# The last RMS statistic: its root moved from GpSimd to ScalarE and VectorE, its final products all on VectorE

## The chip, the core and the metric

One core of a Trainium2 chip runs the whole program. The metric is the time of one execution on the device in microseconds (us), the median of several runs. Engines are TensorE (PE; its weight loads are PEld), VectorE (DVE), ScalarE (ACT), GpSimd (POOL) and SyncE (SP, which issues most DMAs). Each engine works through its own list of instructions in order; semaphores hold an instruction back until what it needs from another engine is done.

## What is computed

One step of a two-layer network on 640 tokens (512 latent, 128 context) of width 1024. Each layer has a token mixer (attention, then a gated linear recurrence) and a SwiGLU block, each with an RMS norm in front and a gated residual behind. This case is about the very end: the down-projection of the last block, its residual, and the final RMS norm of every token:

```python
def _rms_norm(x, g):
    xf = x.astype(jnp.float32)
    y = xf * lax.rsqrt(jnp.mean(xf * xf, axis=-1, keepdims=True) + RMS_EPS)
    return (y * g.astype(jnp.float32)).astype(x.dtype)
...
        lat = lat + g2_l[:, None, :] * f_l
    y_prompt = _rms_norm(ctx, final_g)
    y_sample = _rms_norm(lat, final_g)
```

## The kernel before

The residual stream `x` is kept with features on the 128 partitions: 8 feature chunks (`KT = 8`) by 640 tokens. A mean over features is thus a sum over partitions and over the 8 chunks. ScalarE squares each chunk, the squares are added up chunk by chunk in `ssq`, and `stat` (line 376) lets TensorE multiply the sum by a column of ones: tokens come out on partitions, one column per block of 128 tokens (tile `at`). The last squares are not added but given to the same matmuls as further parts (`lastq`). VectorE makes `var` of it (divide by 1024, add epsilon), GpSimd raises it to the power -0.5 (`rs`, line 389), VectorE spreads the result on a diagonal (`dg`), and TensorE multiplies the diagonal by a square of ones, which puts the root of each token on all partitions, in PSUM (tile `mx`, line 394).

`project_last` (line 451) is the tail. It takes the tokens in two chunks, a (0 to 384) and b (384 to 640). For a it runs the 8 products of TensorE with the down weights, one for each feature chunk, with residual (line 425) and square (line 371), then `stat`. For b it runs the 8 products again; beside them the final products of a (`final`, line 465) are placed, each of them `x` times gain times root. In b, ScalarE squares each chunk (line 477, tiles `ssq` and `snap`), GpSimd adds the squares of chunks 1 to 5 (line 479), and those of 6 and 7 go into the statistic as parts. ScalarE also scales chunks 6 and 7 of b by the gain (line 482). After b's `stat`, ScalarE copies the root out of PSUM (`g`, line 490), because GpSimd can't read there; VectorE does the final products of chunks 0 to 5 of b (line 497), GpSimd those of 6 and 7 (line 499). Stores to HBM go from SyncE's queue in pairs of feature chunks (`store`, line 468): four of a (384 KB each) and four of b (256 KB each).

Which instruction stands where in an engine's list is decided by a scheduler from the program's order and its dependencies; `tc.issue_after(i)` keeps an instruction behind `i`. All engines end at line 1205, the end of the program: each runs a DRAIN and then a barrier. ScalarE works with one table of functions at a time; a function of another table needs an ACT_TABLE_LOAD first, which the build puts in by itself.

Of the kernel before, what the change touches and what calls it, by code (L numbers as in the profile page):

```python
# [9 lines left out]
F32 = mybir.dt.float32  # L10
F32R = mybir.dt.float32r
AF = mybir.ActivationFunctionType
ALU = mybir.AluOpType
AX = mybir.AxisListType

P = 128
D = 1024
KT = D // P
# [22 lines left out]
HT = NTOK // 2  # L41
# [84 lines left out]
class _Step:  # L126
# [235 lines left out]
    def square(self, k, t0, t1):  # L362
        nc = self.nc
        s = slice(t0, t1)
        if k == 0:
            if t0 == 0:
                self.ssq = self.t([P, NTOK], F32, "ssq", 1, self.sb)
            nc.scalar.activation(self.ssq[:, s], self.x[:, k, s], AF.Square)
            return
        q = self.t([P, 384], F32, "sq", 2, self.sb)[:, :t1 - t0]  # L370
        nc.scalar.activation(q, self.x[:, k, s], AF.Square)
        if k < KT - 1:
            nc.vector.tensor_tensor(self.ssq[:, s], self.ssq[:, s], q, ALU.add)
        self.lastq[t0] = [q]

    def stat(self, t0, t1):
        nc = self.nc
        bl = [min(b, t1 - P) for b in range(t0, t1, P)]
        n = len(bl)
        ps = self.ps()  # L380
        parts = [(self.ssq, 0)] + [(q, t0) for q in self.lastq.get(t0, ())]
        for i, (q, o) in enumerate(parts):
            for j, b in enumerate(bl):
                self.at = nc.tensor.matmul(ps[:, j:j + 1], q[:, b - o:b - o + P], self.ones[:, 0:1], start=i == j == 0,
                                           stop=i == len(parts) - 1, skip_group_check=True).ins
        v = self.t([P, 8], F32, "var", 2)[:, 0:n]
        self.var = nc.vector.tensor_scalar(v, ps[:, 0:n], 1.0 / D, EPS, ALU.mult, ALU.add).ins  # L387
        r = self.t([P, 8], F32, "rs", 2)[:, 0:n]
        self.pw = nc.gpsimd.tensor_tensor(r, v, self.mhalf.broadcast_to([P, n]), ALU.pow).ins  # L389
        dg = self.t([P, 4, P], F32, "dg", 1, self.sb)[:, 0:n]  # L390
        self.dg = nc.vector.tensor_tensor(dg, self.ident.unsqueeze(1).broadcast_to([P, n, P]), r.unsqueeze(2).broadcast_to([P, n, P]), ALU.mult).ins
        ps = self.ps("rr" if "rr" in self.ptags else "mx")
        for j, b in enumerate(bl):
            mm = nc.tensor.matmul(ps[:, b - t0:b - t0 + P], self.ones, dg[:, j], start=True, stop=True)
        self.r = ps, t0
        return mm.ins
# [54 lines left out]
    def project_last(self, w, hi, lo, gk):  # L451
        nc, tc = self.nc, self.tc
        G = self.need(self.gcols, gk)
        us = []
        for f in range(0, KT, 2):
            us += self.two(w[f:f + 2], f % 4)
        (a0, a1), (b0, b1) = CHL
        for f, u in enumerate(us):
            self.residual(f, a0, a1, self.chunk(u, hi, lo, a0, a1), G, True)
        mm = self.stat(a0, a1)  # L460
        r0 = self.r[0][:, 0:a1 - a0]

        def final(k):
            xs = self.x[:, k, a0:a1]
            nc.vector.scalar_tensor_tensor(xs, xs, self.col("fg", k), r0, ALU.mult, ALU.mult)

        def store(k, t0, t1):
            nc.sync.dma_start(self.o["y"][k * P - P:k * P + P, t0:t1].rearrange("(k p) t -> p k t", p=P), self.x[:, k - 1:k + 1, t0:t1])

        squares = []  # L470
        for f, u in enumerate(us):
            with tc.issue_after(mm) if f == KT - 1 else nullcontext():
                ps = self.chunk(u, hi, lo, b0, b1)
            last = self.residual(f, b0, b1, ps, G, False)
            xs = self.x[:, f, b0:b1]
            q = self.ssq[:, b0:b1] if f == 0 else self.t([P, HT], F32, "snap", 3, self.sb)[:, 0:b1 - b0]
            nc.scalar.activation(q, xs, AF.Square)
            if 0 < f < KT - 2:
                nc.gpsimd.tensor_tensor(self.ssq[:, b0:b1], self.ssq[:, b0:b1], q, ALU.add)
            squares.append(q)  # L480
            if f >= KT - 2:
                nc.scalar.activation(xs, xs, AF.Copy, scale=self.col("fg", f))
            if 1 < f < KT - 1:
                with tc.issue_after(last):
                    final(f - 2)
        self.lastq[b0] = squares[KT - 2:]
        self.stat(b0, b1)
        r1 = self.r[0][:, 0:b1 - b0]
        rs = self.t([P, HT], F32, "g", 3, self.sb)[:, 0:b1 - b0]
        nc.scalar.copy(rs, r1)  # L490
        with tc.issue_after(self.dg):
            for k in range(KT - 3, KT):
                final(k)
        for k in range(KT):
            xs = self.x[:, k, b0:b1]
            if k < KT - 2:
                nc.vector.scalar_tensor_tensor(xs, xs, self.col("fg", k), r1, ALU.mult, ALU.mult)
            else:
                nc.gpsimd.tensor_tensor(xs, xs, rs, ALU.mult)
        for k in (1, 3):  # L500
            store(k, a0, a1)
        for t0, t1, ks in ((b0, b1, (1,)), (a0, a1, (5, 7)), (b0, b1, (3, 5, 7))):
            for k in ks:
                store(k, t0, t1)
# [704 lines left out]
```

## Time and profile before

| | |
|---|---|
| time, median of 3 runs | 1558.96 us (1558.88 to 1559.05) |
| time of the profiled execution | 1559.64 us |
| its span, first to last instruction of the program | 1557.9 us |
| mean granted clock of TensorE | 0.982 |
| busy: PE, DVE, ACT, POOL | 1491.1, 1076.2, 719.0, 214.0 us |

A row of a timeline is: start and length in us, engine, line, operation, output tile <- input tiles, shapes, count of merged instructions, and in brackets the engine's idle time before it with what ended it. A row of a group is: line, engine, operation, tiles, shapes, count | busy us, mean ns of one | idle time before and its releaser. A row of one line's instructions has the count, then the shortest, median and longest duration in ns, then the first and the last start in us. An engine's name with a small q (SPq, POOLq) is the engine's sequencer, which runs DMA issues, waits and the DRAINs at the program's end.

### The profile page before, as it was taken

To read this page: it belongs to the slowest core of one execution; us is meant where nothing else is said; L and a number is where in the kernel's file an instruction comes from. 1 tells how busy PE (TensorE), PEld (TensorE's weight loads), DVE (VectorE), ACT (ScalarE), POOL (GpSimd) and SP (SyncE) were. 2 spreads that over 40 slices of the span, in tenths; PEclk is the share of its full clock that TensorE was granted. 3 is DMA by queue.
4 is the path that set the end of the run, shared out by engine and by line. 5 is a ranking of instruction groups with operands and counts; after the bars stand their busy time and mean duration, and the time that the engine had idled before them with its cause. 6 is when DMAs were issued, how large, how long until landed. Compare 5 with 4: busy or idle time off the path is not lost.

```text
span 1557.9 us, 26058 instructions
## 1 busy us (share of the span) xinstructions
PE 1491.1 (96%) x10307; PEld 1444.9 (93%) x10307; DVE 1076.2 (69%) x2035; ACT 719.0 (46%) x1329; POOL 214.0 (14%) x238
## 2 busy tenths in 40 slices
PE   6999999989999999999999999969989999999996
PEld 4899999879999999999999888869989999999996
DVE  5678788959999886444446489875876666555645
ACT  4576667654332123212334389764634342424232
POOL 2211122100111110000000000000132323232311
PEclk8999999999999999999999999989999999999998
DMA  9545655535666663222223112124242231313111
GB/s 377 157 114 165 178 167 164 154 122 188 189 191 189 203 194 116 71 82 82 62 84 114 62 58 72 55 97 152 70 142 70 82 109 55 109 55 109 55 55 68
DMA packets 69754, 188.25 MB, mean 121 GB/s; under 512 B 7793, under 2 KB 23297, under 8 KB 69505
## 3 DMA queue, kind: packets, MB, share of 16 engines
q1 hardware_dynamic: 57824, 144.49, 29.5%
q0 software_dynamic: 11520, 41.95, 8.7%
q8 instruction: 81, 1.33, 0.3%
q14 instruction: 41, 0.33, 0.1%
q10 hardware_dynamic: 288, 0.16, 0.0%
HBM read 171.09 MB, written 8.92 MB: 116 GB/s over the span
## 4 chain that ended last, share of the span: by engine, by line
PE 80%; DVE 8%; ACT 7%; DMA 2%; issue 2%; POOL 0%; SPq 0%; DVEq 0%; POOLq 0%; ACTq 0%
PE mm L210 13%; PE mm L209 13%; PE mm L211 13%; PE mx L211 5%; PE mx L210 5%; PE mx L209 5%; PE mx L819 3%; PE mx L821 3%; PE mx L820 3%; PE op L665 2%; PE tp L589 2%; PE mc L819 1%; PE mc L820 1%; PE mc L821 1%; DVE big L1057 1%
## 5 line engine op out<-in xcount | busy, mean ns | idle before, releaser
L209 PE MATMUL mm<-big,whi 128*128 128x320 f32 (+2 forms) x1290 | 402.4, 315 | 16.4 <-ACT big L1056 9.1
L210 PE MATMUL mm<-big,whi 128*128 128x320 f32 (+2 forms) x1290 | 405.0, 314 | 1.7 <-DVE big L1057 1.3
L211 PE MATMUL mm<-big,wlo 128*128 128x320 f32 (+2 forms) x1290 | 403.7, 314 | 1.2 <-DVE wlo L178 1.2
L209 PEld LDWEIGHTS mm<-big,whi 128*128 128x128 f32 x1290 | 245.3, 191 | 21.2 <-ACT big L1056 9.9
L210 PEld LDWEIGHTS mm<-big,whi 128*128 128x128 f32 x1290 | 246.5, 191 | 5.0 <-DVE big L1057 3.7
L211 PEld LDWEIGHTS mm<-big,wlo 128*128 128x128 f32 x1290 | 246.0, 191 | 2.8 <-DVE wlo L178 1.7
L239 DVE SCALAR_TENSOR_TENSOR mprod<-mraw,csb 128x1024 f32<-128x1024 f32 x160 | 195.3, 1221 | 14.3 <-DMA mraw<-in_wm 13.8
L177 ACT CAST whi<-raw 128x1024 fp32r<-128x1024 f32 (+1 forms) x89 | 92.3, 1037 | 112.1 <-PE mm L210 80.5
L425 DVE SCALAR_TENSOR_TENSOR x<-mm,G,x 128x128 f32<-128x128 f32 (+3 forms) x211 | 84.9, 434 | 84.7 <-PE mm L211 83.4
L178 DVE TENSOR_TENSOR wlo<-raw,whi 128x1024 fp32r<-128x1024 f32 (+1 forms) x89 | 108.9, 1224 | 28.4 <-ACT whi L177 26.0
L211 PE MATMUL mm<-big,wlx 128*128 128x320 f32 (+3 forms) x363 | 112.7, 311 | 0.0
L210 PE MATMUL mm<-big,whx 128*128 128x320 f32 (+3 forms) x363 | 112.6, 310 | 0.0
L209 PE MATMUL mm<-big,whx 128*128 128x320 f32 (+3 forms) x363 | 112.4, 310 | 0.0
L235 POOL DMA_DIRECT2D mraw<-in_wm x80 | 43.5, 544 | 384.1 <-DVE mprod L239 269.7
L209 PE MATMUL mx<-big,whi 128*128 128x320 f32 (+3 forms) x278 | 87.0, 313 | 0.9 <-DVE big L674 0.9
L389 POOL TENSOR_TENSOR rs<-var,mhalf 128x3 f32<-128x3 f32 (+3 forms) x10 | 9.2, 928 | 568.8 <-DVE var L387 568.8
L211 PE MATMUL mx<-big,wlo 128*128 128x320 f32 (+3 forms) x278 | 86.9, 312 | 0.0
L210 PE MATMUL mx<-big,whi 128*128 128x320 f32 (+3 forms) x278 | 86.8, 312 | 0.0
L177 ACT CAST whx<-raw 128x1024 fp32r<-128x1024 f32 (+1 forms) x39 | 40.0, 1027 | 88.5 <-PE mm L210 54.7
L211 PE MATMUL mx<-big,wlx 128*128 128x320 f32 (+3 forms) x245 | 76.2, 311 | 0.2 <-DVE wlx L178 0.2
L210 PE MATMUL mx<-big,whx 128*128 128x320 f32 (+3 forms) x245 | 76.1, 310 | 0.0
L209 PE MATMUL mx<-big,whx 128*128 128x320 f32 (+3 forms) x245 | 76.0, 310 | 0.0
(292 smaller groups left out, 3622.7 us busy)
## 6 DMA issues: line engine op xcount, KB each, us to landing
raw<-in_gu SPq DMA_DIRECT2D x88, 512.0 KB, 3.6
mraw<-in_wm POOLq DMA_DIRECT2D x80, 512.0 KB, 3.9
raw<-in_dn SPq DMA_DIRECT2D x24, 512.0 KB, 3.7
raw<-in_wqk SPq DMA_DIRECT2D x16, 512.0 KB, 5.1
raw<-in_wi SPq DMA_DIRECT2D x16, 512.0 KB, 3.5
raw<-in_dn SPq DMA_DIRECT2D x16, 448.0 KB, 3.3
sw<-in_wm SPq DMA_DIRECT2D x10, 512.0 KB, 10.9
raw<-in_wv SPq DMA_DIRECT2D x8, 512.0 KB, 3.9
```

The lines of the kernel that those rows point to most:

```text
L177: nc.scalar.copy(hi, raw)
L178: nc.vector.tensor_tensor(lo, raw, hi.bitcast(F32), ALU.subtract)
L209: nc.tensor.matmul(ps, hi[:, k], xhi[:, k, s], start=(k == 0), stop=False)
L210: nc.tensor.matmul(ps, hi[:, k], xlo[:, k, s], start=False, stop=False)
L211: nc.tensor.matmul(ps, lo[:, k], xhi[:, k, s], start=False, stop=(k == nk - 1))
L235: nc.gpsimd.dma_start(w, self.i["wm"][l * 6 + j - 2, f])
L239: nc.vector.scalar_tensor_tensor(prod, w, 1.0, self.csb[:, s], ALU.mult, ALU.mult, accum_out=out[:, s, f:f + 1])
L425: last = self.nc.vector.scalar_tensor_tensor(xs, ps[:, a - t0:b - t0], G[:, s, f:f + 1], xs, ALU.mult, ALU.add).ins
L589: nc.tensor.transpose(tp[:, j * P:j * P + P], s[:, j * P:j * P + P], self.ident)
L819: nc.tensor.matmul(ps, hi[:, k], xh[:, k], start=start and k == 0, stop=False, skip_group_check=not start)
L820: nc.tensor.matmul(ps, hi[:, k], xl[:, k], start=False, stop=False, skip_group_check=not start)
L821: nc.tensor.matmul(ps, lo[:, k], xh[:, k], start=False, stop=(k == KH - 1), skip_group_check=not start)
```

## The change

It is confined to the tail. `stat` gets a flag `root`, which only the very last statistic sets. With it, the power on GpSimd is replaced by a square root on ScalarE and, on VectorE, a reciprocal `y` and one Newton step `y (1.5 - 0.5 v y y)`. The table of the square root is loaded early, by a dummy square root that is kept behind the last square of chunk a. GpSimd loses three kinds of work: the fifth add of squares (chunk 5's square is now a third part of the statistic, which is two more matmuls of one column), the power, and the final products of chunks 6 and 7, which go to VectorE. With them ScalarE loses the two scalings by the gain and the copy of the root. The final product of chunk 5 of a is placed ahead of the last statistic and not behind it.

```diff
     def square(self, k, t0, t1):
...
-        nc.scalar.activation(q, self.x[:, k, s], AF.Square)
+        self.sqr = nc.scalar.activation(q, self.x[:, k, s], AF.Square).ins
...
-    def stat(self, t0, t1):
+    def stat(self, t0, t1, root=False):
...
         r = self.t([P, 8], F32, "rs", 2)[:, 0:n]
-        self.pw = nc.gpsimd.tensor_tensor(r, v, self.mhalf.broadcast_to([P, n]), ALU.pow).ins
+        if root:
+            y, z = [self.t([P, 8], F32, m, 1)[:, 0:n] for m in ("ry", "rz")]
+            nc.scalar.activation(y, v, AF.Sqrt)
+            nc.vector.reciprocal(y, y)
+            nc.vector.tensor_tensor(z, v, y, ALU.mult)
+            nc.vector.scalar_tensor_tensor(z, z, -0.5, y, ALU.mult, ALU.mult)
+            nc.vector.scalar_tensor_tensor(r, z, 1.5, y, ALU.add, ALU.mult)
+        else:
+            self.pw = nc.gpsimd.tensor_tensor(r, v, self.mhalf.broadcast_to([P, n]), ALU.pow).ins
...
             self.residual(f, a0, a1, self.chunk(u, hi, lo, a0, a1), G, True)
+        with tc.issue_after(self.sqr):
+            nc.scalar.activation(self.t([P, 1], F32, "dum", 1), self.ones[:, 0:1], AF.Sqrt)
         mm = self.stat(a0, a1)
...
-            if 0 < f < KT - 2:
+            if 0 < f < KT - 3:
                 nc.gpsimd.tensor_tensor(self.ssq[:, b0:b1], self.ssq[:, b0:b1], q, ALU.add)
             squares.append(q)
-            if f >= KT - 2:
-                nc.scalar.activation(xs, xs, AF.Copy, scale=self.col("fg", f))
-            if 1 < f < KT - 1:
+            if f > 1:
                 with tc.issue_after(last):
                     final(f - 2)
-        self.lastq[b0] = squares[KT - 2:]
-        self.stat(b0, b1)
+        self.lastq[b0] = squares[KT - 3:]
+        self.stat(b0, b1, True)
         r1 = self.r[0][:, 0:b1 - b0]
-        rs = self.t([P, HT], F32, "g", 3, self.sb)[:, 0:b1 - b0]
-        nc.scalar.copy(rs, r1)
         with tc.issue_after(self.dg):
-            for k in range(KT - 3, KT):
+            for k in range(KT - 2, KT):
                 final(k)
         for k in range(KT):
             xs = self.x[:, k, b0:b1]
-            if k < KT - 2:
-                nc.vector.scalar_tensor_tensor(xs, xs, self.col("fg", k), r1, ALU.mult, ALU.mult)
-            else:
-                nc.gpsimd.tensor_tensor(xs, xs, rs, ALU.mult)
+            nc.vector.scalar_tensor_tensor(xs, xs, self.col("fg", k), r1, ALU.mult, ALU.mult)
```

Ahead of the tail the lists of all engines are the same as before. VectorE's list at its end, from the last products of a beside b's residuals to the end of the program, before:

```order
L465 SCALAR_TENSOR_TENSOR x_10897<-x_10897,cols_61,mx_15878 128x384
L387 TENSOR_SCALAR var_16036<-at_16029 128x2 [waits PE_49]
L391 TENSOR_TENSOR dg_16040<-ident_63,rs_16038 128x256 [waits Pool_49]
L465 SCALAR_TENSOR_TENSOR x_10897<-x_10897,cols_61,mx_15878 128x384 x2
L465 SCALAR_TENSOR_TENSOR x_10897<-x_10897,cols_61,mx_15878 128x384 [waits Activation_49]
L497 SCALAR_TENSOR_TENSOR x_10897<-x_10897,cols_61,mx_16042 128x256 [waits Activation_49]
L497 SCALAR_TENSOR_TENSOR x_10897<-x_10897,cols_61,mx_16042 128x256 [waits DVE_49]
L497 SCALAR_TENSOR_TENSOR x_10897<-x_10897,cols_61,mx_16042 128x256
L497 SCALAR_TENSOR_TENSOR x_10897<-x_10897,cols_61,mx_16042 128x256 [waits DVE_49]
L497 SCALAR_TENSOR_TENSOR x_10897<-x_10897,cols_61,mx_16042 128x256 x2
```

The same place of VectorE's list in the changed kernel, whose lines stand 8 to 10 further down (line 475 there is line 465 here, line 502 is line 497; `ry` and `rz` are the new small tiles):

```order
L475 SCALAR_TENSOR_TENSOR x_10897<-x_10897,cols_61,mx_15880 128x384 x2
L387 TENSOR_SCALAR var_16038<-at_16029 128x2 [waits PE_49]
L392 RECIPROCAL ry_16041<-ry_16041 128x2 [waits Activation_49]
L393 TENSOR_TENSOR rz_16042<-var_16038,ry_16041 128x2 [waits DVE_49]
L394 SCALAR_TENSOR_TENSOR rz_16042<-rz_16042,ry_16041 128x2 [waits DVE_49]
L395 SCALAR_TENSOR_TENSOR rs_16040<-rz_16042,ry_16041 128x2 [waits DVE_49]
L399 TENSOR_TENSOR dg_16048<-ident_63,rs_16040 128x256 [waits DVE_49]
L475 SCALAR_TENSOR_TENSOR x_10897<-x_10897,cols_61,mx_15880 128x384 x2
L502 SCALAR_TENSOR_TENSOR x_10897<-x_10897,cols_61,mx_16050 128x256 [waits PE_49]
L502 SCALAR_TENSOR_TENSOR x_10897<-x_10897,cols_61,mx_16050 128x256 x7
```

One product of a moved ahead of `var`, four small instructions stand between `var` and `dg`, each waiting for the one before, and the products of b are eight and wait for TensorE.

GpSimd's list at its end, from the power of chunk a's statistic on, as the difference (lines 389 and 397 are the power; 479 and 489 the adds):

```order
-L389 TENSOR_TENSOR rs_15874<-var_15872,mhalf_68 128x3 [waits DVE_49]
-L479 TENSOR_TENSOR ssq_15745<-ssq_15745,snap_15913 128x256 [waits PE_49,Activation_49]
-L479 TENSOR_TENSOR ssq_15745<-ssq_15745,snap_15931 128x256 [waits Activation_49,Pool_49]
-L479 TENSOR_TENSOR ssq_15745<-ssq_15745,snap_15950 128x256 [waits Activation_49,Pool_49]
-L479 TENSOR_TENSOR ssq_15745<-ssq_15745,snap_15969 128x256 [waits Activation_49,Pool_49]
-L479 TENSOR_TENSOR ssq_15745<-ssq_15745,snap_15988 128x256 [waits Activation_49,Pool_49]
-L389 TENSOR_TENSOR rs_16038<-var_16036,mhalf_68 128x2 [waits DVE_49]
-L499 TENSOR_TENSOR x_10897<-x_10897,g_16045 128x256 [waits Activation_49]
-L499 TENSOR_TENSOR x_10897<-x_10897,g_16045 128x256
```

```order
+L397 TENSOR_TENSOR rs_15876<-var_15874,mhalf_68 128x3 [waits DVE_49]
+L489 TENSOR_TENSOR ssq_15745<-ssq_15745,snap_15915 128x256 [waits PE_49,Activation_49]
+L489 TENSOR_TENSOR ssq_15745<-ssq_15745,snap_15933 128x256 [waits Activation_49,Pool_49]
+L489 TENSOR_TENSOR ssq_15745<-ssq_15745,snap_15952 128x256 [waits Activation_49,Pool_49]
+L489 TENSOR_TENSOR ssq_15745<-ssq_15745,snap_15971 128x256 [waits Activation_49,Pool_49]
```

The fourth add is GpSimd's last instruction now; behind it stands only the end of the program.

ScalarE's list at its end in the changed kernel, from the last squares of a (line 371) to the root (line 391):

```order
L371 ACTIVATE sq_15863<-x_10897 128x384 [waits DVE_49]
L469 ACT_TABLE_LOAD
L469 ACTIVATE dum_15865<-ones_72 128x1
L487 ACTIVATE ssq_15745<-x_10897 128x256 [waits DVE_49]
L487 ACTIVATE snap_15915<-x_10897 128x256 [waits DVE_49]
L487 ACTIVATE snap_15933<-x_10897 128x256
L487 ACTIVATE snap_15952<-x_10897 128x256 [waits DVE_49]
L487 ACTIVATE snap_15971<-x_10897 128x256 [waits Pool_49]
L487 ACTIVATE snap_15990<-x_10897 128x256 [waits Pool_49]
L487 ACTIVATE snap_16008<-x_10897 128x256 [waits DVE_49,Pool_49]
L487 ACTIVATE snap_16026<-x_10897 128x256 [waits Pool_49]
L391 ACTIVATE ry_16041<-var_16038 128x2 [waits DVE_49]
```

The table load and the dummy stand ahead of the first square of b; the two scalings and the copy that stood at the list's end are gone, and the root is there alone.

## The prediction

> **What bounds the kernel now.** I read the page first, to see what kind of time this is, then only the last 15 us, where every changed line stands.
>
> ```profile
> span 1557.9 us, 26058 instructions
> PE 80%; DVE 8%; ACT 7%; DMA 2%; issue 2%; POOL 0%; SPq 0%; DVEq 0%; POOLq 0%; ACTq 0%
> ```
>
> The span is a TensorE span: four fifths of the chain that ended last are matmuls, and the change touches none of the work in front of about 1528 us. So the question is the tail: how long after the last product of TensorE the program ends. The windows of that tail show who is still at work:
>
> ```profile
> 1544.00:1546.00 2.00, 1.50 (x12) 1.41 (x12) 0.82 (x3) 1.52 (x4) 0.24 (x1) 1.00 0.44 167
> 1546.00:1548.60 2.60, 1.20 (x4) 0.93 (x4) 1.80 (x4) 0.00 (x0) 0.70 (x1) 0.59 0.00 0
> 1548.60:1551.50 2.90, 0.00 (x0) 0.00 (x0) 2.64 (x7) 0.37 (x1) 1.41 (x2) 0.50 0.96 345
> 1551.50:1557.90 6.40, 0.00 (x0) 0.00 (x0) 0.00 (x0) 0.00 (x0) 0.00 (x0) 0.50 0.38 130
> ```
>
> The columns are the length, then busy time of PE, PEld, DVE, ACT and POOL, the granted clock, the DMA share and GB/s. First the sum of squares (PE 1.50), then root and broadcast, then 2.9 us of products with the DMA engines full (0.96), then 6.4 us in which no engine computes. That last stretch is the longest of the four. The instructions of line 1205 (the end of the program: each engine's DRAIN, then a barrier) say what it waits for:
>
> ```profile
> L1205 SPq DRAIN  x2: 7/7/7, 1554.5 to 1554.6; - x2
> L1205 DVEq DRAIN  x1: 2468/2468/2468, 1549.0 to 1549.0; - x1
> L1205 POOLq DRAIN  x3: 40/93/8072, 1549.0 to 1557.6; - x3
> L1205 POOLq EVENT_SEMAPHORE  x4: 17/17/17, 1557.1 to 1557.8; - x4
> ```
>
> SyncE, which waits for every store, is through at 1554.6. VectorE's DRAIN begins at 1549.0 and takes 2.47, so to 1551.5: exactly to the end of its last product. GpSimd's begins at 1549.0 too but takes 8.07, to 1557.1, and only then does the barrier start; from there to the end it is 0.8 us. So for 2.5 us (1554.6 to 1557.1) **the program waits for GpSimd's DRAIN alone**, and that, not the products, ends the span. GpSimd's late work is this:
>
> ```profile
> 1542.69 0.74 POOL L479 TENSOR_TENSOR ssq<-ssq,snap 128x256 f32<-128x256 f32 x1
> 1541.87 2.36 POOL L479 TENSOR_TENSOR ssq<-ssq,snap 128x256 f32<-128x256 f32 x3 [0.40 <-ACT snap L477]
> 1546.07 0.70 POOL L389 TENSOR_TENSOR rs<-var,mhalf 128x2 f32<-128x2 f32 x1 [1.83 <-DVE var L387]
> 1549.06 1.41 POOL L499 TENSOR_TENSOR x<-x,g 128x256 f32<-128x256 f32 x2 [2.29 <-ACT g L490]
> ```
>
> Its last products end at 1550.47; the DRAIN holds on for 6.6 us more. Nothing in the trace says why. The two other DRAINs of GpSimd, behind no work, take 0.04 and 0.09, so it is something that its work leaves behind.
>
> **The change, part by part.** *The sum of squares.* PE and VectorE there:
>
> ```profile
> 1544.29 0.61 PE L384 MATMUL at<-ones,ssq 128*128 128x1 f32 x4 [0.80 <-POOL ssq L479]
> 1544.76 1.03 PE L384 MATMUL at<-ones,snap 128*128 128x1 f32 x8
> 1544.23 0.72 ACT L477 ACTIVATE snap<-x 128x256 f32<-128x256 f32 x2 [1.88 <-POOL ssq L479]
> 1545.83 0.16 DVE L387 TENSOR_SCALAR var<-at 128x2 f32<-128x2 f32 x1 [1.17 <-PE at L384]
> ```
>
> Before, PE starts at 1544.29 behind GpSimd's fifth add (ends 1544.23). After, the fifth add is gone and two matmuls (four records) read that square directly; the running sum is ready at 1543.43, behind the fourth add. The first eight records fit before 1544.6. The last eight need the squares of chunks 6 and 7; the first of those ends near 1544.65 (each takes 0.42), so 1544.70 plus 1.03 gives 1545.73 instead of 1545.79. Gain 0.05: ScalarE's square is late next, right behind the removed add.
>
> *The root.* Before, var ends at 1545.99 and dg starts at 1546.80, so GpSimd's power costs 0.81 with its hand-overs. After, one ScalarE instruction and four dependent VectorE ones stand there. The trace has no such root; nearest are these rows (two scales of 128x2, a reciprocal of 128x2, a dependent chain of 128x16, and the slowest op of 128x2):
>
> ```profile
> L983 ACT ACTIVATE xr<-bias 128x2 f32<-128x2 f32 x16 | 3.1, 193 | 0.3 <-ACT r L419 0.2
> L613 DVE RECIPROCAL sm<-sm 128x2 f32<-128x2 f32 x8 | 1.3, 162 | 5.5 <-ACT S L612 5.5
> 66.02 0.18 DVE L957 TENSOR_TENSOR l_pl<-l_pl,l_z 128x16 f32<-128x16 f32 x1
> 66.23 0.18 DVE L958 TENSOR_SCALAR l_pl<-l_pl 128x16 f32<-128x16 f32 x1
> L610 DVE TENSOR_SCALAR mx<-mx 128x2 f32<-128x2 f32 x8 | 2.7, 336 | 0.1
> ```
>
> 0.19 for the root with 0.03 on each side, 0.20 for the reciprocal with its gap, three times 0.21 (66.02 to 66.23): 1.08, so 0.27 **slower** than the power. The ends: five ops with no gap, 0.19 + 4 x 0.16 = 0.83, or +0.02; four at 0.336 with 0.04 each and 0.25 for ScalarE, 1.75, or +0.94. I take the near one. ScalarE's root has nothing queued behind it; behind VectorE's waiting reciprocal stand dg, for which PE's broadcast waits, and all products. So dg starts at 1546.80 - 0.05 + 0.27 = 1547.02.
>
> *The table load.* It is queued on ScalarE behind the last square of the first token chunk. ScalarE is idle there:
>
> ```profile
> 1529.19 0.42 ACT L477 ACTIVATE ssq<-x 128x256 f32<-128x256 f32 x1 [0.22 <-DVE x L425]
> 1539.42 0.72 ACT L477 ACTIVATE snap<-x 128x256 f32<-128x256 f32 x2 [9.81 <-DVE x L425]
> 905.81 1.28 ACT L1027 ACT_TABLE_LOAD   x1
> 907.11 1.28 ACT L1027 ACTIVATE lt<-lt 128x1286 f32<-128x1286 f32 x1
> ```
>
> Load (1.28) and dummy (taken as 0.19, like the scales above) push one square from 1529.19 to about 1530.6; its reader, GpSimd's first add, needs the next square too, which ends after 1539.8. The 9.81 of idle time hide it; cost nothing. Without that cover it would be 1.3.
>
> *Broadcast and products.*
>
> ```profile
> 1546.80 0.42 DVE L391 TENSOR_TENSOR dg<-ident,rs 128x256 f32<-128x256 f32 x1 [0.82 <-POOL rs L389]
> 1547.38 1.20 PE L394 MATMUL mx<-dg,ones 128*128 128x128 f32 x4 [1.58 <-DVE dg L391]
> 1547.15 1.66 DVE L465 SCALAR_TENSOR_TENSOR x<-x,cols,mx 128x384 f32<-128x384 f32 x3
> 1548.61 0.37 ACT L490 COPY g<-mx 128x256 f32<-128x256 f32 x1 [2.86 <-PE mx L394]
> 1549.01 2.44 DVE L497 SCALAR_TENSOR_TENSOR x<-x,cols,mx 128x256 f32<-128x256 f32 x6 [0.21 <-ACT g L490]
> ```
>
> From dg's start to the end of the broadcast it is 1.78 (1546.80 to 1548.58), unchanged: 1548.80. Beside it VectorE now has two first-chunk products instead of three (0.35 + 0.53 + 0.61, done by 1548.5), so they delay nothing. Before, the last products wait for ScalarE's copy and start 0.43 behind the broadcast; after, they wait for PE alone, 0.03 (as the copy did, 1548.58 to 1548.61), so 1548.83: 0.18 earlier than 1549.01. But there are eight and not six: six take 2.44, one alone 0.47, so 0.394 from start to start, and eight take 7 x 0.394 + 0.47 = 3.23. They end at 1552.06 against 1551.45: **0.61 later**. The two scalings on ScalarE (line 482) and the two products on GpSimd went beside other work; dropping them gains nothing here.
>
> *The stores.* The rows are: the product of chunk 4, the two late stores of the first token chunk, the last store, and the time from issue to landing of the last store and of the first one of the second token chunk:
>
> ```profile
> 1544.05 0.61 DVE L465 SCALAR_TENSOR_TENSOR x<-x,cols,mx 128x384 f32<-128x384 f32 x1
> 1547.78 1.42 SPq L468 DMA_DIRECT2D out_y<-x  x2
> 1551.52 0.44 SPq L468 DMA_DIRECT2D out_y<-x  x1
> DMA to landing us min/median/max: 2.9/2.9/2.9
> DMA to landing us min/median/max: 2.2/2.2/2.2
> ```
>
> It lands at 1554.42 after 2.9, since the DMA engines are full (0.96 above): the two late stores of the first token chunk go out from 1547.78, just ahead of the four last ones. After, the product of chunk 5 follows that of chunk 4 (1544.05 + 0.53 + 0.61 = 1545.2), so their store leaves early, and the other goes at 1548.5. The last four follow 0.79 apart. I take 2.2 for the last (the least loaded row), 2.9 as upper end: issue 1552.10, landing 1554.30 (to 1555.0). SyncE is through 0.2 behind it as before: 1554.5.
>
> *GpSimd's end.* Its DRAIN began when the first of its last two products started. After, its last work is the fourth add, so its DRAIN begins at 1542.7, and with the same 8.07 ends at 1550.8, or counted from the end of the work (1543.43 + 6.6) at 1550.1. Either is 3.7 us before SyncE, which is late next.
>
> **The sum.** Barrier from 1554.5, plus 0.8: 1555.3 against 1557.9, so -2.6. The profiled execution took 1559.64, that is 1.74 around its span; less 2.6 it is 1557.0. It stands 0.68 over the median of the runs, 1558.96, so the median becomes **1556.4**. By the ends of root and landing: 1556.1 to 1557.8.
>
> By the Trainium skill, "VectorE: DVE Perf Modes", section "The DRAIN you can't avoid", the DRAINs of the closing sequence are constant, about 12 ns on all engines. By that rule GpSimd's would hold nothing up itself, and something else would keep the barrier: the first rival, 1558.9. The rows of SyncE (7 ns) agree, the one of 8072 ns does not.
>
> **The rivals.** (1) *The wait only looks like GpSimd's.* If what the DRAIN waits for follows the stores (1557.09 is 2.67 behind the last landing), the end is 1554.30 + 2.67 + 0.8, so 1557.8: -0.1, or 1558.9. For it: nothing named ends the wait, and GpSimd's results were out at 1550.5. Against: the other engines' DRAINs end with their own work. 0.10.
> (2) *Slower: the DRAIN follows VectorE.* If GpSimd can't finish while VectorE works, it ends 5.64 behind VectorE's last product (1557.09 - 1551.45). With eight products that is 1552.06 + 5.64 = 1557.70: +0.6, or 1559.6, up to 1560.2 by the upper end of the root. It decides as soon as it passes SyncE's 1554.5. Against: VectorE's own DRAIN ends at once. 0.07.
> (3) *The load isn't hidden*, or comes a second time in front of the root: 1.3 on the path, 1557.7. The order of instructions shows one load only, in the idle stretch. 0.04.
> By the Trainium skill, "ScalarE: Activation LUTs", section "What ACT_TABLE_LOAD costs", a switch costs 2.66 us with a drain; by it rival 3 would give 1559.1. The load above is followed by the next ACTIVATE after 1.30, so no run here shows the rest.
>
> **How the numbers follow.** The forecast has 0.75, the rivals 0.10, 0.07 and 0.04, something unseen 0.04. A measurement of this kernel can tell some 0.2% from no change, 3.1 us: faster begins under 1555.8, slower over 1562.1. The forecast's gain is 0.17%, so nearly all cases count as no change that can be told; faster gets 0.08 (the forecast with a tail shorter than its lower end), slower 0.03 (most of the unseen), the same 0.89. The range goes from 1555.8 to 1558.9, past the forecast's own 1556.1 to 1557.8, to take in rivals 1 and 3; rival 2, faster and the unseen stay out, 0.18 to 0.19 together.
>
> **What would show it.** GpSimd's long DRAIN starts near 1542.7 and ends before SyncE's at 1554.5; span near 1555.3; dg some 0.2 later; eight products ending near 1552.1; the last landing within 2.2 to 2.9 of its issue; one table load near 1529. The forecast is wrong if GpSimd's DRAIN still ends after SyncE's, or if the statistic waits for ScalarE by more than 0.5.

## The result, and the profile after

The changed kernel takes 1554.93 us (median of 18 runs, 1552.54 to 1560.27), against 1560.10 (18 runs, 1556.07 to 1564.47) for the kernel before in the same series: ratio 0.9968, 95% interval 0.9957 to 0.9979, so 5 us or 0.3% faster. The forecast was 1556.4, in a range from 1555.8 to 1558.9; the change gained more than it allowed for. The three runs that the forecast started from, within 0.2 us of each other, were no measure of the spread.

The profiled execution of the changed kernel took 1558.85, with this span and chain:

```profile
span 1557.0 us, 26068 instructions
PE 81%; DVE 8%; ACT 6%; DMA 2%; issue 2%; POOL 0%; SPq 0%; DVEq 0%; ACTq 0%; POOLq 0%
```

By its span it is only 0.9 us shorter than the one before, where 2.6 were forecast. It must not be read so. TensorE's last product with the down weights ends at 1543.49 in the profile of before (1544.29 less the 0.80 of idle time in the row of line 384) and at 1545.34 in this one (the row of line 211 in the next fence). I call what comes behind that moment the *tail*: 1557.87 - 1543.49 = 14.38 before, 1557.03 - 1545.34 = **11.69 after, 2.69 less**. Everything ahead of it is the same list of instructions, and took 1.85 longer in this execution.

The timeline of the tail, on the engines that the change touches (start, length, engine, line, operation, tiles):

```profile
1543.84 1.55 POOL L489 TENSOR_TENSOR ssq<-ssq,snap 128x256 f32<-128x256 f32 x2
...
1545.06 0.28 PE L211 MATMUL mx<-big,wlx 128*128 128x256 f32 x1
...
1545.92 1.69 PE L384 MATMUL at<-ones,snap 128*128 128x1 f32 x12
...
1547.64 0.16 DVE L387 TENSOR_SCALAR var<-at 128x2 f32<-128x2 f32 x1 [0.61 <-PE at L384]
1547.84 0.20 ACT L391 ACTIVATE ry<-var 128x2 f32<-128x2 f32 x1 [1.03 <-DVE var L387]
1548.08 0.17 DVE L392 RECIPROCAL ry<-ry 128x2 f32<-128x2 f32 x1 [0.27 <-ACT ry L391]
1548.28 0.16 DVE L393 TENSOR_TENSOR rz<-var,ry 128x2 f32<-128x2 f32 x1
1548.47 0.16 DVE L394 SCALAR_TENSOR_TENSOR rz<-rz,ry 128x2 f32<-128x2 f32 x1
1548.67 0.16 DVE L395 SCALAR_TENSOR_TENSOR rs<-rz,ry 128x2 f32<-128x2 f32 x1
1548.86 0.42 DVE L399 TENSOR_TENSOR dg<-ident,rs 128x256 f32<-128x256 f32 x1
...
1549.43 1.20 PE L402 MATMUL mx<-dg,ones 128*128 128x128 f32 x4 [1.83 <-DVE dg L399]
1550.67 3.22 DVE L502 SCALAR_TENSOR_TENSOR x<-x,cols,mx 128x256 f32<-128x256 f32 x8 [0.33 <-PE mx L402]
```

From `var` to `dg` it is 1547.80 to 1548.86, and the eight products fill 3.22 us without a gap. The end of the program (line 1208 now: count, then shortest, median and longest in ns, then first and last start) and the last two stores:

```profile
L1208 POOLq EVENT_SEMAPHORE  x4: 17/17/17, 1556.3 to 1556.9; - x4
L1208 POOLq DRAIN  x3: 40/93/7397, 1544.6 to 1556.8; - x3
L1208 SPq DRAIN  x3: 7/7/7, 1556.2 to 1556.5; - x3
...
L1208 DVEq DRAIN  x2: 19/1634/3249, 1550.7 to 1556.5; - x2
```

```profile
L478 SPq DMA_DIRECT2D out_y<-x x2: 372/372/373, 1553.1 to 1553.9; - x2
...
DMA to landing us min/median/max: 2.2/2.2/2.2
```

GpSimd's DRAIN is still long (7.40) but begins at 1544.6 and is over at 1552.0, 6.62 behind its last add (1545.39). VectorE's last product ends at 1553.89, its store lands 2.2 after its issue, SyncE is through at 1556.3, and the barrier follows at once. The end of the program now hangs on the stores and not on GpSimd. On ScalarE the table load stands where it was expected:

```profile
1530.86 1.28 ACT L469 ACT_TABLE_LOAD   x1
1532.15 0.20 ACT L469 ACTIVATE dum<-ones 128x1 f32<-128x1 f32 x1
1532.26 0.40 ACT L487 ACTIVATE ssq<-x 128x256 f32<-128x256 f32 x1
1541.71 0.42 ACT L487 ACTIVATE snap<-x 128x256 f32<-128x256 f32 x1 [9.05 <-DVE x L433]
```

So the tail did what was forecast, and half of the measured gain is somewhere else. That is what most of the experiments are about.

### The profile page after: what moved, and what is told of

Its sections match the earlier page's. It is cut to its first block, busy times and chain, and to the rows that moved or that the text cites. A ratio compares the mean times of both kernels' runs of the same rounds, so it can differ in the third digit from the quotient of the medians.

```text
span 1557.0 us, 26068 instructions
## 1 busy us (share of the span) xinstructions
PE 1496.7 (96%) x10311; PEld 1448.3 (93%) x10311; DVE 1079.6 (69%) x2041; ACT 719.7 (46%) x1329; POOL 206.5 (13%) x234
## 4 chain that ended last, share of the span: by engine, by line
PE 81%; DVE 8%; ACT 6%; DMA 2%; issue 2%; POOL 0%; SPq 0%; DVEq 0%; ACTq 0%; POOLq 0%
PE mm L210 13%; PE mm L209 13%; PE mm L211 13%; PE mx L211 5%; PE mx L209 5%; PE mx L210 5%; PE mx L822 3%; PE mx L823 3%; PE mx L824 3%; PE op L668 2%; PE tp L592 2%; PE mc L822 1%; PE mc L823 1%; PE mc L824 1%; DVE big L1060 1%
## 5 line engine op out<-in xcount | busy, mean ns | idle before, releaser
L239 DVE SCALAR_TENSOR_TENSOR mprod<-mraw,csb 128x1024 f32<-128x1024 f32 x160 | 195.8, 1224 | 15.4 <-DMA mraw<-in_wm 14.8
L397 POOL TENSOR_TENSOR rs<-var,mhalf 128x3 f32<-128x3 f32 (+2 forms) x9 | 8.5, 950 | 568.0 <-DVE var L387 568.0
```

The costliest lines, as they stand in the source:

```text
L239: nc.vector.scalar_tensor_tensor(prod, w, 1.0, self.csb[:, s], ALU.mult, ALU.mult, accum_out=out[:, s, f:f + 1])
```

## The experiments

All kernels of one call ran on one chip beside runs of the kernel before (154 runs, in five calls, with medians of 1560.43 to 1561.59). *Shift* is how far about half of all tiles (`x` and `whx` among them; `big` and `raw` stay) stand further in SBUF than before; it is read from the addresses in the built programs. A tail is that of one profile, and one kernel's tails differ: 14.38, 14.42 and 14.01 for the kernel before, 11.69 three times and 11.50 for the changed one, 2.6 apart on average.

| label | shift, bytes | tail, us | median | mean (runs) | mean clock |
|---|---|---|---|---|---|
| after | 64 | 11.69 | 1554.93 | 1555.49 (18) | 0.986 |
| e1_control | 0 | 14.42 | 1560.21 | 1560.00 (12) | 0.983 |
| e2_repeat | 64 | 11.69 | 1555.39 | 1555.20 (11) | 0.985 |
| e3_shift | 64 | 14.02 | 1559.62 | 1559.54 (12) | 0.982 |
| e4_late_pool | 64 | 16.22 | 1560.30 | 1559.59 (12) | 0.983 |
| e5_power | 0 | 11.51 | 1559.19 | 1559.35 (12) | 0.982 |
| e6_table | 0 | 14.78 | 1561.92 | 1561.25 (12) | 0.982 |
| e7_control2 | 0 | 14.01 | 1560.24 | 1561.23 (12) | 0.982 |
| e8_repeat2 | 64 | 11.69 | 1556.07 | 1556.12 (12) | 0.984 |
| e9_root_only | 64 | 14.26 | 1560.44 | 1559.86 (12) | 0.983 |
| e10_copy_for_root | 64 | 11.52 | 1556.40 | 1556.05 (12) | 0.984 |
| e11_idle_power | 64 | 11.68 | 1556.85 | 1556.83 (9) | 0.984 |
| e12_no_shift | 0 | 11.69 | 1557.42 | 1558.69 (12) | 0.983 |
| e13_power_shift | 64 | 11.69 | 1555.26 | 1555.92 (7) | 0.985 |
| e14_shift_repeat | 64 | 14.00 | 1559.35 | 1558.88 (12) | 0.984 |
| e15_shift128 | 128 | 14.38 | 1559.45 | 1560.42 (12) | 0.982 |
| e16_no_shift2 | 0 | 11.52 | 1558.13 | 1558.21 (12) | 0.984 |
| e17_repeat3 | 64 | 11.50 | 1554.75 | 1555.26 (12) | 0.985 |
| e18_power2 | 0 | 11.53 | 1558.72 | 1558.84 (12) | 0.983 |

### First call: GpSimd's drain, and is the tail all?

e1 and e2 are the two kernels unchanged. e3 adds tiles that nothing uses to the kernel before, e4 a late small add on GpSimd to the changed one:

```diff
 e3_shift (to the kernel before)
+        for m in ("ry", "rz"):
+            self.t([P, 8], F32, m, 1)
 e4_late_pool (to the changed kernel, behind the products of b)
+        late = self.x[:, KT - 1, b0:b0 + 8]
+        nc.gpsimd.tensor_tensor(self.t([P, 8], F32, "ry", 1), late, late, ALU.add)
```

> The kernel before, unchanged. Both theories: ratio 1.000 to itself; from the start of the last 'at' weight load's predecessor (the last product of TensorE) to the end of the span 14.4 us as before. It shows how far a ratio of this size of sample strays with nothing changed: theory A (the change acts in the tail alone, -2.7 us, and the rest of the measured -5.2 us is the spread of the time ahead of the tail) needs a stray of 1 to 3 us (0.1 to 0.2%) to be usual; theory B (something ahead of the tail became some 2.4 us faster too) needs it to be under 1 us.

> The changed kernel, unchanged. Theory A: the tail from TensorE's last product to the end is 11.7 us again, 2.7 shorter than before, and the ratio is near 0.9983 (-2.7 us) on another sample, so between 0.997 and 0.9995. Theory B: tail the same, but the ratio comes back at 0.9968 (-5 us).

> The kernel before with two unused small tiles allocated where the change allocates its two: every large tile then lies 64 bytes further in SBUF, as in the changed kernel, and no instruction differs. Theory A: ratio 1.000, 0 us but for the spread. Theory B, if the addresses are what made the time ahead of the tail shorter: -2.4 us, ratio 0.9985, with the tail at 14.4 us as before.

> The changed kernel with one more GpSimd add of 128x8 elements (its result is not used), which waits for the last product of VectorE. GpSimd's DRAIN ended 6.62 us behind its last instruction in both profiles so far. Theory A: the late add ends some 0.2 us behind VectorE's last product, the DRAIN 6.6 us later, some 4.3 us behind SyncE's, and the program ends 4.3 us later than the changed kernel: tail 16.0 us, +1.6 us against the kernel before, ratio near 1.001. Rival (the DRAIN's wait belongs to the stores or to VectorE and not to GpSimd's own work): tail 11.7 us as in the changed kernel, -2.7 us.

e4's GpSimd at the end, from its timeline and its row of line 1210:

```profile
1551.24 0.20 POOL L504 TENSOR_TENSOR ry<-x 128x8 f32<-128x8 f32 x1 [8.67 <-DVE x L502]
```

```profile
L1210 POOLq EVENT_SEMAPHORE  x4: 17/17/17, 1558.1 to 1558.7; - x4
L1210 POOLq DRAIN  x3: 40/93/6861, 1551.2 to 1558.6; - x3
```

An add of 0.20 us, placed last, holds the program until 1551.2 + 6.86 = 1558.1, 6.6 behind its end; the tail grows by 4.53. That GpSimd's drain follows its own last work is shown, and rivals 1 and 2 fall with it. But the sums don't close: by the tails, e4 should be 1.8 us over the controls and was level with them, and e2 should be 2.7 under e1 and was 4.8 under it. All three kernels with the change were some 2 us too fast *ahead* of the tail. e3 had no clear answer (0.9985, 95% 0.9969 to 1.0002). e1, the kernel before itself, came out at 0.9988 (0.9974 to 1.0002), its mean 2.0 us under that of the other runs of the same kernel: the stray that theory A of its expectation needs does occur with nothing changed.

### Second and third call: which part of the change?

```diff
 e5_power (to the changed kernel): no early load, power on GpSimd again
-        with tc.issue_after(self.sqr):
-            nc.scalar.activation(self.t([P, 1], F32, "dum", 1), self.ones[:, 0:1], AF.Sqrt)
-        self.stat(b0, b1, True)
+        self.stat(b0, b1)
 e6_table (to the kernel before): early load alone
+        with tc.issue_after(self.sqr):
+            nc.scalar.activation(self.t([P, 1], F32, "dum", 1), self.ones[:, 0:1], AF.Sqrt)
 e9_root_only (to the kernel before): early load as in e6, and the new root
-        self.stat(b0, b1)
+        self.stat(b0, b1, True)
 e10_copy_for_root (to the changed kernel): no early load, and
-            nc.scalar.activation(y, v, AF.Sqrt)
+            nc.scalar.activation(y, v, AF.Copy)
 e11_idle_power (to the changed kernel): beside the new root
+            nc.gpsimd.tensor_tensor(self.t([P, 8], F32, "rs", 2)[:, 0:n], v, self.mhalf.broadcast_to([P, n]), ALU.pow)
```

e7 and e8 are again the two kernels unchanged.

> The changed kernel with the last root taken back to GpSimd's power (no square root, no table load, no Newton step); GpSimd still has no late add and no late products. Theory A (only the tail matters, and the drain ends 6.62 us after GpSimd's last operation): the power ends some 3.2 us after TensorE's last product, so the drain ends at +9.9, before SyncE's at +10.7; the root takes 0.81 instead of 1.06, so the tail is 11.4 to 11.5, 0.25 shorter than the changed kernel's 11.69 and 2.9 shorter than 14.4 before. Rival (the drain costs as soon as GpSimd works on the last statistic at all): tail 14 or more. Theory B1 (the square root's table or instructions are also what made the time ahead of the tail some 2 us shorter): the run is then 1.7 us slower than e8_repeat2; without B1 it is equal or 0.25 faster.

> The kernel before with the early table load and its dummy square root added, nothing else. Theory A: hidden in ScalarE's idle time, tail 14.4, time equal to e7_control2 within 0.1%. Theory B1 (this load is what made the time ahead of the tail shorter): 2 us faster than e7_control2, with a granted clock 0.002 higher. Rival 3 of the prediction (the load isn't hidden): 1.3 us slower.

> The kernel before, unchanged, as a second control. Theory C (the time ahead of the tail differs from run to run by spells of half clock that come by chance, and is the same for all these kernels in the mean): tail 14.4, median within 1.5 us of the runs of before in this call, and 2.7 us above e8_repeat2. Theory B (the changed kernel is faster ahead of the tail too): 4.5 us above e8_repeat2.

> The changed kernel, unchanged, last in its call and not second. Tail 11.69. Theory C: 2.7 us below e7_control2. Theory B: 4.5 us or more below it, as e2_repeat was below e1_control.

> The kernel before with only the root of the last statistic changed (early table load, square root, reciprocal, Newton step); GpSimd keeps its fifth add and its two last products. By the rows of the root the tail is 0.25 longer than 14.4, 14.6 to 14.7, and the drain again ends 6.62 us behind GpSimd's last product. Theory C (time ahead of the tail the same in the mean): median 0.2 us over the runs of before. Theory B2 (the new root makes the time ahead of the tail shorter, by the early load, by the square root, or by the power that is gone): 2 to 3 us below the runs of before.

> The changed kernel with ScalarE's square root replaced by a copy and without the early load: the square root is left out of the computation, everything else stands as it is. Tail 11.6 to 11.7. If the square root or its table made the time ahead of the tail shorter: 1557.5 to 1558, 2 to 3 us over the changed kernel's 1555 to 1556. If it is GpSimd's late power that made it longer, or neither: 1555 to 1556.

> The changed kernel with GpSimd's power of the last statistic computed beside the new root into a tile that nobody reads. It ends 3.2 us after TensorE's last product, so the drain ends at +9.9, before SyncE's at +10.9: tail 11.69, unchanged. If GpSimd's late power is what makes the time ahead of the tail longer: 1557.5 to 1558.5. If the square root makes it shorter, or neither: 1555 to 1556.

The tails came as expected within 0.5 us. e5's drain begins with the power and ends 6.62 behind it, at +9.87, before SyncE at +10.76: the power on GpSimd costs nothing by the drain. e11's idle power shows the same:

```profile
1547.46 0.71 POOL L396 TENSOR_TENSOR rs<-var,mhalf 128x2 f32<-128x2 f32 x1 [2.46 <-DVE var L387]
```

```profile
L1209 POOLq EVENT_SEMAPHORE  x4: 17/17/17, 1555.9 to 1556.5; - x4
L1209 POOLq DRAIN  x3: 40/93/7367, 1547.4 to 1556.3; - x3
```

Its drain is over at 1554.8, and the barrier's first row is at 1555.9. Ahead of the tail it was a puzzle: e5, without the root, lost the extra gain (1559.19) although its tail is the shortest; e10, without square root and table, kept most of it (1556.40); e6, with the table alone, had none; e11, with a late power, kept most. No single operation fits. What did fit was not an operation: the root's two small tiles `ry` and `rz` push half of all tiles 64 bytes further, and after, e2, e4, e8 to e11 have that shift, e1, e5, e6 and e7 don't.

### Fourth and fifth call: 64 bytes

```diff
 e12_no_shift, e16_no_shift2 (to the changed kernel): ry and rz in the free half of dg
-            y, z = [self.t([P, 8], F32, m, 1)[:, 0:n] for m in ("ry", "rz")]
+            dt = self.t([P, 4, P], F32, "dg", 1, self.sb)
+            y, z = dt[:, 2, 0:n], dt[:, 3, 0:n]
 e13_power_shift (to e5_power), e14_shift_repeat (to the kernel before)
+        for m in ("ry", "rz"):
+            self.t([P, 8], F32, m, 1)
 e15_shift128 (to the kernel before)
+        for m in ("ry", "rz", "u0", "u1"):
+            self.t([P, 8], F32, m, 1)
```

e17 is the changed kernel, e18 is e5_power.

> The changed kernel with the two small tiles of its new root kept inside the free half of the tile dg, so that no other tile's SBUF address moves against the kernel before; same instructions. Tail 11.69 in either case. Theory L (the changed kernel's two new tiles push about half of all tiles 64 bytes further in SBUF, and that makes the time ahead of the tail 2 to 3 us shorter): this kernel loses it, 1557.5 to 1558.5. Theory R (the new root's instructions make it): 1555 to 1556, as the changed kernel.

> e5_power (power on GpSimd, no late add, no late products) with two tiles added that nothing uses, so that its other tiles stand 64 bytes further, as in the changed kernel. Tail 11.5. Theory L: 1554.5 to 1556, 3 us below e5_power's 1559.2. Theory R: as e5_power, 1558 to 1559.5. Neither (e5_power's median was a draw): 1557.

> e3_shift again: the kernel before with the 64 bytes of shift alone. Tail 14.0 to 14.4. Theory L: 2 to 3 us below the runs of before in this call (1557.5 to 1558.5). Theory R: equal to them.

> The kernel before with four unused tiles: 128 bytes of shift. Tail 14.0 to 14.4. Theory L with 64 bytes as an alignment: equal to the runs of before. Theory L with any distance: 2 to 3 us below them. Theory R: equal to them.

> e12_no_shift again (the changed kernel, its new tiles placed so that nothing moves in SBUF), beside the changed kernel in one call. Theory L: 2 to 2.5 us above e17_repeat3, granted clock 0.002 lower, tail 11.69. Theory R: equal to e17_repeat3.

> The changed kernel, unchanged. Tail 11.69, median 1555 to 1556 by all theories.

> e5_power again (power on GpSimd, nothing moves in SBUF). Tail 11.5 to 11.7. Theory L: equal to e16_no_shift2 within 0.5 us, both 2 to 2.5 us above e17_repeat3 and e13_power_shift. Theory R: 2.5 us above e16_no_shift2.

e16, e17 and e18 ran side by side. The changed kernel with its addresses put back loses 3.4 us (1558.13 against 1554.75), with the tail and the work unchanged, and is then level with e18, which has no new root (1558.72). The expected size, 2 to 2.5, was too small. With the shift and without the root's instructions, e13 is as fast as the changed kernel (1555.26), 3.9 under e5, whose program differs from e13's in nothing but addresses. e5 ran in another call; e12, in the call of e13, has the new root without the shift, and its mean is 2.8 above (1558.69 against 1555.92). So **in the changed kernel the place of the tiles, and not the root's instructions, makes the rest of the gain**. For the kernel before it is less sure: e14, with the shift alone, is 1.8 under the runs of before (ratio 0.9979, 95% 0.9964 to 0.9995), of which 0.4 is its tail, and by means e1 strayed by 2.0 with nothing changed, where e14 is 2.5 under. 128 bytes gave no gain that can be told (0.9991, 95% 0.9973 to 1.0010), but this interval holds e14's 0.9979 too: that the distance matters, and not that something moved, isn't shown.

The size, by means less each kernel's tail: eleven kernels with 64 bytes have 1543.4 to 1545.6, on average 1544.4; eight with 0 or 128, and the kernel before in its six series, have 1545.6 to 1547.8, on average 1546.8. That is 2.4 us, and with 2.7 for the tail it makes 5.1, where 5.0 was measured (1560.47 less 1555.49 by the means). It is not one fixed amount, though: among the kernels with GpSimd's late products (with the shift e3, e9 and e14) it is 1.4, and 1.0 against e1, e6, e7 and e15 alone; among the others it is 3. Why that is, the runs don't show. e13 doesn't beat the changed kernel, and no other version does.

### How 64 bytes can cost 2 us

The clock rows show where some of the time goes. Two profiles at the same place of the program, e18 first, then e17. The columns are the stretch, its length, then busy time of PE, PEld, DVE, ACT and POOL, the granted clock of TensorE, the DMA share and GB/s:

```profile
862.90:866.30 3.40, 3.40 (x16) 3.40 (x15) 0.23 (x2) 0.00 (x0) 0.16 (x1) 0.50 0.00 0
866.30:869.70 3.40, 3.40 (x14) 3.40 (x14) 0.56 (x1) 0.16 (x1) 1.55 (x2) 0.50 0.02 5
```

```profile
856.60:860.00 3.40, 3.40 (x26) 3.40 (x25) 0.23 (x2) 0.00 (x0) 0.47 (x1) 1.00 0.05 20
860.00:863.40 3.40, 3.40 (x25) 3.40 (x24) 0.56 (x1) 0.16 (x1) 1.24 (x2) 1.00 0.02 5
```

The same work beside it (0.23 and 0.56 on VectorE), but 30 matmuls at half clock in the one against 51 at full clock in the other. Such spells last 3.41 us or a multiple, and within one profile their starts lie whole multiples of 3.413 apart (in the profile of before, 27.6, 327.9 and 857.0: the last two stand 88 and 243 of them behind the first). Where that grid lies against the program's start differs from one execution to the next. Whether a pause of TensorE costs a spell depends on where it falls in the grid. One is the wait for the diagonal of the first chunk's statistic, always 1.17 long; its row in the profile of before, and the two cells of the grid around it:

```profile
1535.33 0.94 PE L394 MATMUL mx<-dg,ones 128*128 128x128 f32 x6 [1.17 <-DVE dg L391]
```

```profile
1532.80:1536.20 3.40, 2.23 (x18) 2.03 (x19) 1.24 (x4) 0.00 (x0) 0.86 (x1) 1.00 0.00 0
1536.20:1539.60 3.40, 3.40 (x18) 3.40 (x17) 1.22 (x3) 0.18 (x1) 0.00 (x0) 0.51 0.02 5
```

And in e17:

```profile
1534.09 0.94 PE L402 MATMUL mx<-dg,ones 128*128 128x128 f32 x6 [1.17 <-DVE dg L399]
```

```profile
1531.90:1535.30 3.40, 2.23 (x18) 2.03 (x19) 1.47 (x5) 0.00 (x0) 0.85 (x1) 1.00 0.02 5
1535.30:1538.70 3.40, 3.40 (x31) 3.40 (x30) 1.79 (x6) 0.89 (x3) 1.00 (x2) 1.00 0.00 0
```

The pause begins 0.39 of a cell behind a grid line in the first, 0.28 in the second. In all 20 profiles: from 0.39 to 0.77 (14 of them) the next cell runs at half clock, from 0.24 to 0.36 (6 of them) it doesn't. One such cell costs up to half of 3.41, 1.7 us (18 matmuls in it, not 31). Measured it is 1.6: from the last VectorE instruction that writes `wlx`, near 1508 us, to TensorE's last product it is 34.97 to 35.12 us in the 14 profiles and 33.45 to 33.54 in the 6. By the Trainium skill, "TensorE: Matmul & The Clock Gate", section "Part 1: The HAM clock gate", the clock is granted by a window of 3413 ns that runs freely and does not restart with the kernel; the trace agrees (3.41).

Ahead of the tail the profiles have 34 to 58 us at half clock. The eleven with 64 bytes have 40.6 on average, the nine without 46.3; half of the difference is 2.8, and the last product ends 2.3 earlier in them (1542.4 against 1544.7). The mean granted clock of all runs tells the same among kernels of like tails: 0.9849 with the shift against 0.9829 without, for those with tails of 11.5 to 11.7 (81 and 48 runs), and 0.9830 against 0.9821 for those with 14.0 to 14.8 (36 and 48 runs, the runs of before left out). Of 1557 us that is 3.1 and 1.4, near the two sizes above. So the shift goes with fewer half-clock spells, and they are large enough for the whole of its gain.

That they are the cause of all of it is argued, not shown. The sum of half-clock time doesn't tell how long an execution is: the profiles of after and e2, of one kernel, both have 37.6 us of it ahead of the tail, and their last products end at 1545.34 and 1538.65. It counts where a spell falls, and executions differ by other things too. At the same VectorE instruction near 50 us, e2 has had 10.2 us at half clock and after none, and e2 is 3.1 ahead. Between the same VectorE instructions near 364 and 700 us, near 836 and 894, and from 1508 to the last product, the time does follow the spells, and these three stretches together are 2.4 shorter on average with the shift, all others together 0.1 longer. But few profiles carry that: three of the nine without the shift have a spell in the first stretch and none of the eleven with it, three against one in the second, eight against six in the third. No stretch carries the difference in every profile, and why addresses change the number of spells is open.

## Why the prediction was off, step by step

- *Bound: GpSimd's DRAIN.* Right. It ends 6.62 us behind GpSimd's last operation in all 20 profiles (6.63 in one), whether that is an add, a power or a product. The reading "counted from the end of the work" was the exact one.
- *Sum of squares.* From the last product to the end of the `at` matmuls 2.27 against 2.30: 0.03 gained, forecast 0.05.
- *Root.* 1.06, forecast 1.08: VectorE's four and `dg` follow 0.20 apart, with gaps of 0.03.
- *Table load.* Hidden: the square behind it is done at 1532.66, its reader starts after 1541.71. e6, which adds the load alone, came out at 0.9998 (95% 0.9985 to 1.0011).
- *Products.* They start 0.04 behind the broadcast and take 3.22, forecast 0.03 and 3.23.
- *Stores.* Landing 2.2, as taken.
- *Sum.* Tail -2.69, forecast -2.6. With the last product 1.85 later in this execution, the forecast span of 1555.3 becomes 1557.1; it was 1557.0.
- **The step that failed** is the first one: "the change touches none of the work in front of about 1528 us". That is true of the instructions, and the order on every engine confirms it, but not of the addresses. Two new tiles of 32 bytes a partition moved about half of all tiles, and the time ahead of the tail fell by about 2.4 us (3 for kernels with the tail of the changed one), which no term of the sum had. None of the rivals had it either.
- *The median.* Taking 2.6 off a median of three runs gave 1556.4. Later runs of the kernel before had medians of 1560.1 to 1561.6, so the starting value was 1.1 to 2.6 us low; that error had the other sign and by luck hid part of the failed step. From 1560.10 the same sum gives 1557.5, and the changed kernel with nothing moved took 1557.42 and 1558.13 (e12, e16).

## What to carry to other kernels

When a trace shows an engine's closing DRAIN ending after the last store, take away that engine's late work, however small: what counts is when its last operation ends. A change of a few us in a kernel of 1.5 ms can't be read off the spans of two profiles; cut both at a common event, and compare the parts. And a new tile, however small, is a change to the whole kernel when it moves the others: before giving the gain to the instructions that use it, run them with nothing moved (as e16) and the move without them (as e13).

## What was not expected of the hardware

- GpSimd's DRAIN ends 6.62 us behind its last operation, constant to 0.01 over 20 profiles; behind no work it takes 0.04 to 0.09. By the Trainium skill, "VectorE: DVE Perf Modes", section "The DRAIN you can't avoid", the DRAINs of a profile's preamble and postamble are constant at about 12 ns on all five engines; GpSimd's at the end of this program, 6.86 to 8.07 us in the rows shown, is unlike that.
- In the changed kernel, a shift of 64 bytes of about half the tiles is worth some 3 us of 1558 (e16 against e17, e12 against e13), along with a granted clock 0.002 higher; whether one of 128 bytes is worth anything couldn't be told.
- Whether one pause of 1.17 us is followed by 3.41 us at half clock was decided between 0.36 and 0.39 of the grid's cell, without an exception in 20 profiles (starts from 0.24 to 0.77 were seen).
